# Shifts of attention maxima moved from VectorE to GpSimd under a new hand-written order, and the feature rows of the prologue turned earlier

## The chip, the cores and the metric

The kernel runs on one core of a Trainium2 chip. The metric is the time of one launch on the device in microseconds (us), the median over several runs. A profile of one execution gives every instruction on the engines: TensorE (PE, with its weight loads shown apart as PEld), VectorE (DVE), ScalarE (ACT), GpSimd (POOL), and the queue of the SyncE (SP), which issues nearly all DMAs.

## The reference: what is computed

One trunk layer runs on a group of 128 context tokens and a group of 512 latent tokens with shared weights, all in float32:

```python
def trunk_layer(h, ada, p, rope_tabs, ctx_k, ctx_v):
    sh1, sc1, g1, sh2, sc2, g2 = jnp.split(ada, N_ADA, axis=-1)
    u = rms_norm(h, p["g_pre1"]) * (1 + sc1) + sh1
    mo, k, v = mixer(u, p, rope_tabs, ctx_k, ctx_v)
    h = h + g1 * rms_norm(mo, p["g_post1"])
    u = rms_norm(h, p["g_pre2"]) * (1 + sc2) + sh2
    h = h + g2 * rms_norm(conv_ffn(u, p), p["g_post2"])
    return h, k, v
...
    def one_block(qblk):
        s = jnp.einsum('bqkgd,btkd->bkgqt', qblk, k).astype(jnp.float32) * scale
        p = jax.nn.softmax(s, axis=-1).astype(v.dtype)
        return jnp.einsum('bkgqt,btkd->bqkgd', p, v)
```

`ada` is `silu(c) @ w_ada + b_ada`, six vectors of 1024 for each group. The mixer projects `u` with `w_in`, normalises q and k per head, turns the latent ones by a two-axis rotary, attends (16 query heads, 4 key heads of 64; latent tokens read 512 latent and 128 cached keys, context tokens only the 128 context keys), adds a gated short convolution, and multiplies by `w_o`. A gated feed-forward part of width 2816 follows.

## The kernel before

**Arithmetic.** A matrix product in float32 is made of three products of parts: each operand is cut into an upper part `hi` in a shorter format and a rest `lo`, and `hi*hi + hi*lo + lo*hi` is summed in PSUM. The upper part of a weight is copied by ScalarE (`hi`, L826), the rest subtracted in two halves by VectorE or GpSimd (`lo`, L831).

**Prologue** (L374 to L687, up to about 57 us of the trace). SP loads five tiles of 128 token rows (`XT`), then the first columns of `w_ada` and of `w_in`. ScalarE's own queue loads `rows1`: c, the context vector, the bias `b_ada` and `g_pre1` as 72 rows of 128. TensorE begins with `WARM` = 32 turns of the unit matrix (L379), whose output nobody reads. For each tile t, `square(t)` sums squares on ScalarE (L435) and takes the root on GpSimd (L282, L283), `normal(t)` scales the tile on VectorE (L440), `x_turn(t)` turns its eight blocks on TensorE (L447), and `x_copy` takes the two halves out of PSUM on ScalarE or VectorE (L453, L455). `features()` (L416) turns `rows1` on TensorE (L418) and makes silu of c and of the context vector on ScalarE (L419, L420); `feature_columns()` (L423) copies the turned rows into `feat` on VectorE and adds 1 to two of its groups (L424, L426). `ada1_mm` (L478) multiplies silu(c) with the columns of `w_ada`; its results set `scsh`, with which `modulate` makes `u`. PE, ACT, DVE and SP run here in the order in which the code is written.

**Attention** (L747 to L1233, about 57 to 228 us). Every piece of work has a number in order of its making, a name, an engine (`ways`), the works that it follows and the buffers that it takes. `PLAN` is a text of 944 items, number, letter and digits: the letter picks the way (`a` the first engine, `b` the second, `c` the third), the digits the buffers. `follow` (L722) issues the works in that order, and each engine's own order follows from it; nothing is rearranged later.

- Query tile `qgt` (key head g, tile t): four quarters of six matmuls (`qgt.0` to `.3`, L709), rotary products on VectorE (L849, L850) and a sum of the two (`add`, L870, either engine), squares on ScalarE (L872), sums on VectorE (L874), a factor on GpSimd (L877), the norm (L892, either engine), two turns on TensorE (`qgt turn`, L1034), upper part on ScalarE (L1036) and rest on VectorE (L1038). Key tiles go the same way (norm L882).
- The values are scaled (`v scale`, L975) and cut into halves (L981, L984).
- 36 steps: one for each key head's context tile (n = 0, 9, 18, 27) and two for each of its four latent tiles, with two heads in each. In a step with latent tokens: scores of both heads (`s n`, twelve matmuls, L1073), the negated maximum of each head (L1120, VectorE), for the second head the maximum shifted by 15 ln 2 (L1123), the exponential on ScalarE with that bias and its sum (L1128), the first float16 half of the weights on ScalarE (L1134), the second half (L1139 for the second head, L1141 for the first), a transposing DMA of both halves by SP (L1145), and the value product (`pv n`, L1162 and L1170). Then come the output's scaling and cut (L1182 to L1192).
- `POOL_WAY` has a digit for each of the 32 latent steps: with 1, the second head's exponential goes to a buffer in SBUF and its second half is made by GpSimd; with 0, both stay in PSUM and on VectorE.
- TensorE fills the time between scores and value products with quarters of later query tiles and with two columns of gates.

**Behind it** come the product with `w_att_out`, the other columns of `w_in` and the later products (L1274), in a fixed order, up to the end.

Of the kernel before, what the change touches and what calls it, by code (L numbers as in the profile page):

```python
# [18 lines left out]
ALU = mybir.AluOpType  # L19
# [26 lines left out]
WARM = 32  # L46
# [5 lines left out]
71a0 15a 21a 80a 36a 5b0 31a 72a2 81a 45a 52a3 7a 16a 37b1 82a 22a12 92a2 46a 85a1 73a 8a0 23b 83a10 17a2 54a3 9a 86a 132a 38a1  # L52
10a 27a3 42a01 18a0 39a 93a 55a 19a 43a 40a 28a4 74a 60b2 94a 29a 59b3 95a 87a 75b 20a 105a3 98a0 84a 30a 76a1 106a 88a 77a0 99a
78a 107a 100a 58b4 56a0 47b4 65a 347a2 57a 134b 61a 96a22 48a1 63a 348a 108a 97a 49a 118a0 349a 101a 109a01 119a 133b 50a 89a2
102a1 120a 62a 90a1 209a 111a2 351a1 91a 110a 121a 112a 138a 66a 113a 359a10 352a 124a1 103a2 114a 122a10 204a 353a5 365a 140b
115a4 135a0 116a3 366a 104a 367a0 139b 136a 117a 350a 360a 368a0 373a20 123a 275a 125a 361a 64a 126a 141a 362a4 379a 205b 142a
380a 371a 363a 381a1 354a1 369a 143a2 364a0 382a2 374a 391a10 355a2 144a0 356a 383a 375a 151a0 370a1 145a 397a 357a 152a 376a1
146a 398a 385a 384a2 392a 399a0 153a 377a 147a 393a 154a 358a 206b 405a02 394a3 378a3 155a01 400a4 395a 127a 148a1 157a2 411a
401a 149a0 128a3 372a0 396a4 129a1 412a 158a 413a1 130a 159a 406a 414a0 423a12 403a 402a5 150a 407a 415a 164a1 429a 408a2 165a
156a 430a 281a 409a 431a0 166a 416a0 160a 424a 432a1 167a 417a 425a 433a 437a02 168a20 426a3 435a 386a 170a1 443a 169a 410a1  # L60
444a 427a 177a1 387a2 445a1 388a 178a 438a 389a 428a2 446a4 455a12 390a 171a 439a 447a 404a0 456a 440a0 434a3 449a 457a 441a
172a 418a 461a 458a2 173a 161a2 442a4 419a1 179a 459a 162a2 180a 163a 462a 420a 463a0 469a10 448a5 181a10 464a3 467a 182a 487a2
470a 183a0 421a 465a 190a1 460a0 488a 471a 191a 475a 472a1 192a 422a 210a 184a 466a1 174a0 473a 193a 185a 175a3 489a 176a 476a
186a 194a02 450a0 211a 436a 212a 477a1 474a4 490a 195a 478a0 481a 499a10 196a2 907a 479a 451a1 197a 207a1 491a4 505a 276a 208a
198a 506a 480a5 452a 507a0 492a 213a 199a 500a 453a 513a20 508a2 493a2 454a 278b 501a 468a0 514a 509a 502a3 519a 515a 214a 503a
277b 510a3 516a1 482a 520a 215a2 521a1 517a 187a3 504a0 483a0 511a 525a 531a02 188a1 484a 522a0 189a 518a1 200a3 216a1 523a 537a
485a 494a1 201a0 486a 538a 217a 223a0 495a2 202a 524a4 218a 539a0 496a 224a 532a 497a 219a 540a4 545a12 498a 533a 911a 541a
220a1 551a 534a2 225a 221a2 552a 226a 535a 542a5 553a1 546a 554a3 563a02 227a11 547a 555a 536a2 222a 548a1 557a 512a1 569a 229a0
228a 570a 549a 571a0 526a 556a0 564a 572a0 577a12 543a 230a 527a0 573a 565a 528a 550a3 236a0 583a 529a 566a4 231a 237a 575a 584a
578a 585a1 238a 574a1 567a 232a 586a2 239a 530a 579a 587a 595a20 240a02 568a4 580a3 589a 544a1 242a2 601a 241a 602a 596a 558a  # L70
603a0 588a2 581a 597a 233a0 243a 609a01 234a3 607a 244a 559a1 582a5 235a 604a1 560a 249a0 610a 245a 561a 598a0 250a 562a 605a
611a 599a 246a1 251a 247a1 615a 600a0 612a4 627a2 616a 248a 617a1 252a 628a 606a3 618a2 590a1 621a 613a 255a1 619a 629a 256a
576a 253a20 614a2 257a 254b 639a10 591a2 620a5 630a 631a3 592a 258a 262a0 640a 593a 263a 594a 641a 645a 264a 282a 646a 632a 265a
647a0 633a1 283a 279a1 266a11 284b 642a0 280a 648a1 643a 653a20 267a 915a 268a0 651a 908a 644a4 269a 649a 608a0 654a 659a 655a
622a 270a 909a 650a0 656a4 259a3 660a 271a 661a1 285a 657a 910b 260a0 286a 665a 623a0 658a3 261a 662a2 272a2 624a 671a21 287a0
625a 663a 288a2 626a 273a2 289a 634a1 919a 677a 290a 664a2 295a0 678a 635a2 672a 679a0 291a 296a 274a 673a 636a 685a10 637a 683a
674a3 638a 297a 691a 680a0 298a 681a 692a 675a 693a1 292a1 299a21 676a5 694a1 703a20 686a 300a 301a1 293a3 302a 666a0 695a 687a
682a1 709a 688a4 697a 294a 652a 710a 303a 704a 696a2 711a0 689a 308a1 667a0 304a 705a 668a 717a01 690a3 669a 715a 712a2 670a
309a 706a3 723a 713a 310a 724a 707a 725a1 311a 718a 714a0 726a0 305a0 735a21 312a12 306a1 727a 719a 307a 708a4 684a0 314a0 741a
720a1 313a 742a 721a 698a 743a0 728a1 736a 744a4 749a01 729a 699a1 315a 745a 722a5 737a 700a 321a1 750a 738a2 322a 755a 316a  # L80
751a 746a2 323a 739a 752a3 317a 324a 756a 747a 701a 753a 757a1 767a2 740a3 702a 327a2 716a0 758a0 768a 759a 328a 769a 325a00
779a01 754a0 761a 329a 326b 318a1 780a 730a 319a0 760a4 771a1 330a 320a 781a 772a 334a1 785a 782a4 331a4 335a 773a1 332a2 786a
770a 783a 787a 336a 333a 912a 337a 791a 784a5 793a02 340a1 914a 788a2 338a22 913b 916a 799a 762a1 339a 731a1 800a 732a 801a0
917b 748a 789a 733a 341a 802a3 790a0 918b 811a21 734a 794a 763a0 342a 920a0 764a 795a 817a 921a 803a 765a 796a0 818a 812a 922a
819a1 797a 923a 343a 804a4 813a 766a 825a10 805a 924a 823a 814a1 798a2 774a1 820a4 831a 821a 344a0 832a 815a 833a0 826a 816a3
345a3 843a20 834a2 346a 827a 835a 792a0 822a1 849a 775a2 828a3 850a 776a 806a 851a1 836a0 829a 777a 844a 857a01 807a1 852a0 778a
808a 830a5 845a 925a1 853a 863a 809a 926a 846a1 864a 810a 858a 865a0 927a 854a2 837a 855a 928a 859a 847a 930a0 860a4 869a 848a4
875a12 929a 861a 866a2 824a1 867a 881a 882a 876a 838a 883a 862a1 877a 931a 868a3 878a3 887a 932a 839a0 879a 884a0 933a 889a01
880a0 885a 934a 840a 856a0 841a 895a 886a5 896a 842a 935a2 897a 890a 898a1 936a 891a 899a 937a 892a4 901a 900a2 938a 943a 893a
# [23 lines left out]
def trunk_layer(ctx, tc, x_prompt, x_sample, cache_k, cache_v, c, c_ctx, w_ada, b_ada, g_pre1, g_post1, g_pre2,  # L113
# [260 lines left out]
    with tc.tile_pool(name="pro", bufs=2) as pro, tc.manual_schedule(engines={mybir.EngineType.SP}):  # L374
        warm = pro.tile([128, 1], F32, name="warm", bufs=1)
        S.activation(warm, mhalf[:, 0:1], AF.Silu)
        wps = ps1()
        for _ in range(WARM):
            PE.transpose(wps[:, 0:128], ident, ident)  # L379

        def load_rows(srcs, eng):
# [34 lines left out]
        def features():  # L416
            ptr = ps1()
            PE.transpose(ptr[:, 0:72], rows1, ident[0:72, 0:72])  # L418
            S.activation(svec[:, :, 30], ptr[:, 0:8], AF.Silu)  # L419
            S.activation(svec[:, :, 31], ptr[:, 8:16], AF.Silu)  # L420
            return ptr

        def feature_columns():  # L423
            V.tensor_copy(feat[:, 0:72], ptr1[:, 0:72])  # L424
# [293 lines left out]
    def also(w, eng, do):  # L718
        w.ways.append((eng, do))
        return w  # L720
# [26 lines left out]
    with tc.tile_pool(name="att", bufs=1) as at:  # L747
# [305 lines left out]
        for n, (g, t, pi) in enumerate(steps):  # L1053
# [52 lines left out]
            else:  # L1106
                pts[n], exs = [], []
                for h in hs:
# [10 lines left out]
                    def most(s_of=s_of, mk=mk, h=h):  # L1119
                        V.tensor_reduce(out=mk[:, h:h + 1], in_=s_of(), axis=AX.X, op=ALU.max, negate=True)  # L1120

                    def shifted(mk=mk):
                        V.tensor_scalar(out=mk[:, 1:2], in0=mk[:, 1:2], scalar1=SHIFT * math.log(2), scalar2=None, op0=ALU.add)  # L1123
# [3 lines left out]
                    ex = work(f"exp{n}.{h}", "ACT",  # L1127
                              lambda s_of=s_of, e_of=e_of, mk=mk, h=h: S.activation(e_of(), s_of(), AF.Exp, bias=mk[:, h:h + 1],  # L1128
                                                                                   accum_out=mk[:, 4 + h:5 + h]), [mx], [ar[h]] + [er] * way)
# [1395 lines left out]
```

## Time and profile before

| | |
|---|---|
| median of 3 runs | 1075.21 us (1074.77 to 1075.44) |
| profiled execution, own time | 1074.79 us |
| its span in the trace | 1073.0 us |
| PE busy | 1056.8 us (98%) |
| DVE busy | 899.9 us (84%) |
| ACT busy | 598.4 us (56%) |
| POOL busy | 133.1 us (12%) |
| granted TensorE clock over the span | 0.999 |

The span is the trace's first to last instruction; what lies around it is 1.79 us. An engine's busy time counts its computing instructions; matmuls overlap each other, so a busy TensorE can still hold short waits. "Busy" rows by stretch have for each engine the busy time and the number of instructions, then the granted clock, the DMA engines' busy share and GB/s. Wait rows have the waiting engine and line, what released it, the sum in us, how often, and the longest. Rows of one line have the shortest, median and longest time in ns.

### The profile page before, as it was taken

To read this page: it belongs to the slowest core of one execution; us is meant where nothing else is said; L and a number is where in the kernel's file an instruction comes from. 1 tells how busy PE (TensorE), PEld (TensorE's weight loads), DVE (VectorE), ACT (ScalarE), POOL (GpSimd) and SP (SyncE) were. 2 spreads that over 40 slices of the span, in tenths; PEclk is the share of its full clock that TensorE was granted. 3 is DMA by queue.
4 is the path that set the end of the run, shared out by engine and by line. 5 is a ranking of instruction groups with operands and counts; after the bars stand their busy time and mean duration, and the time that the engine had idled before them with its cause. 6 is when DMAs were issued, how large, how long until landed. Compare 5 with 4: busy or idle time off the path is not lost.

```text
span 1073.0 us, 20652 instructions
## 1 busy us (share of the span) xinstructions
PE 1056.8 (98%) x8216; PEld 995.4 (93%) x8216; DVE 899.9 (84%) x1379; ACT 598.4 (56%) x1057; POOL 133.1 (12%) x162
## 2 busy tenths in 40 slices
PE   8999999999999999999999999999999999999997
PEld 6788898899999999999998789999999999999996
DVE  5699999865498999896599678889999988989897
ACT  5478999942344544445322366645555555546673
POOL 1087676500000000000000020000000000000001
PEclk9999999999999999999999999999999999999999
DMA  9829999962244333223668634434544534436873
GB/s 320 256 82 175 190 168 187 191 147 60 75 123 124 93 103 94 79 79 99 189 188 253 198 131 129 121 116 136 166 131 152 150 122 131 152 116 219 277 275 115
DMA packets 243197, 164.02 MB, mean 153 GB/s; under 512 B 94874, under 2 KB 216214, under 8 KB 243102
## 3 DMA queue, kind: packets, MB, share of 16 engines
q1 hardware_dynamic: 242990, 162.68, 55.5%
q8 instruction: 64, 1.05, 0.4%
q14 instruction: 31, 0.25, 0.1%
q10 hardware_dynamic: 112, 0.04, 0.0%
HBM read 123.31 MB, written 17.36 MB: 131 GB/s over the span
## 4 chain that ended last, share of the span: by engine, by line
PE 90%; DVE 3%; ACT 2%; DMA 1%; POOL 1%; issue 1%; SPq 1%; DVEq 0%; ACTq 0%; POOLq 0%
PE b L1274 47%; PE b L235 10%; PE b L237 10%; PE b L236 9%; PE s L709 4%; PE s L1073 2%; PE s L1170 2%; PE s L235 1%; PE s L237 1%; PE s L1162 1%; PE s L478 1%; DVE marks L1120 1%; PE s L236 1%; PE b L1900 1%; ACT P L1134 1%
## 5 line engine op out<-in xcount | busy, mean ns | idle before, releaser
L1274 PE MATMUL b<-ZBr,whi 128*128 128x320 f32 x688 | 152.1, 309 | 0.0
L1274 PE MATMUL b<-MT,whi 128*128 128x320 f32 x608 | 134.4, 309 | 0.0
L1274 PEld LDWEIGHTS b<-ZBr,whi 128*128 128x128 f32 x688 | 114.9, 188 | 0.1
L1274 PE MATMUL b<-ZBr,wlo 128*128 128x320 f32 x344 | 106.1, 308 | 0.0
L1274 PEld LDWEIGHTS b<-MT,whi 128*128 128x128 f32 x608 | 101.7, 188 | 0.0
L1274 PE MATMUL b<-MT,wlo 128*128 128x320 f32 x304 | 94.0, 309 | 0.0
L1261 ACT ACTIVATE whi<-SUM 128x1024 fp32r<-128x1024 f32 x40 | 42.2, 1055 | 78.3 <-DVE SUM L1813 75.7
L1843 DVE SCALAR_TENSOR_TENSOR Y<-C,cffn,Y 128x642 f32<-128x642 f32 x88 | 77.9, 886 | 0.9
L1261 ACT ACTIVATE whi<-WB 128x1024 fp32r<-128x1024 f32 x38 | 40.2, 1058 | 55.5 <-DVE WB L1368 55.5
L1274 PE MATMUL b<-ZBT,whi 128*128 128x320 f32 x320 | 71.0, 308 | 0.0
L1274 PE MATMUL b<-UL,whi 128*128 128x320 f32 x228 | 70.8, 311 | 0.0
L1274 PE MATMUL b<-UH,wlo 128*128 128x320 f32 x228 | 70.1, 307 | 0.0
L1274 PE MATMUL b<-UH,whi 128*128 128x320 f32 x228 | 69.7, 306 | 0.0
L1282 ACT ACTIVATE p<-b 128x320 f32<-128x320 f32 x78 | 34.1, 437 | 55.3 <-PE b L1274 53.5
L1274 PEld LDWEIGHTS b<-ZBr,wlo 128*128 128x128 f32 x344 | 64.6, 188 | 0.0
L1265 DVE TENSOR_TENSOR wlo<-raw,whi 128x1024 fp32r<-128x1024 f32 (+1 forms) x51 | 50.4, 1020 | 13.4 <-ACT whi L1261 13.4
L1274 PEld LDWEIGHTS b<-MT,wlo 128*128 128x128 f32 x304 | 57.1, 188 | 0.0
L1274 PEld LDWEIGHTS b<-ZBT,whi 128*128 128x128 f32 x320 | 54.2, 188 | 1.6
L1120 DVE TENSOR_REDUCE marks<-s 128x1 f32<-128x640 f32 x64 | 52.1, 817 | 4.0 <-PE s L1073 3.8
L1265 DVE TENSOR_TENSOR wlo<-WB,whi 128x1024 fp32r<-128x1024 f32 x38 | 46.5, 1224 | 8.8 <-ACT whi L1261 8.7
L2355 POOL TENSOR_TENSOR ssqs<-ssqs 128x1 f32<-128x1 f32 x4 | 1.4, 356 | 412.9 <-ACT GJ L2349 412.9
L1261 ACT ACTIVATE whi<-raw 128x1024 fp32r<-128x1024 f32 (+1 forms) x51 | 43.5, 892 | 15.4 <-DMA raw<-in_w_o_dram 12.5
(477 smaller groups left out, 3348.1 us busy)
## 6 DMA issues: line engine op xcount, KB each, us to landing
raw<-in_w_in_dram SPq DMA_DIRECT2D x48, 512.0 KB
RAW<-in_w_up_dram SPq DMA_DIRECT2D x40, 512.0 KB
raw<-in_w_down_dram SPq DMA_DIRECT2D x22, 512.0 KB
GA<-in_w_ada_dram SPq DMA_DIRECT2D x16, 512.0 KB
actd<-Y SPq DMA_DIRECT2D x18, 321.0 KB
actl<-ACTb SPq DMA_DIRECT2D x18, 321.0 KB
A<-actl SPq DMA_DIRECT2D x9, 642.0 KB
A<-actd SPq DMA_DIRECT2D x9, 642.0 KB
```

Source lines behind the costliest of these rows:

```text
L235: PE.matmul(out, ah, bh, start=start, stop=False)
L236: PE.matmul(out, ah, bl, start=False, stop=False)
L237: PE.matmul(out, al, bh, start=False, stop=stop)
L709: PE.matmul(out, a, b, start=start and n == 0, stop=stop and n == 2, skip_group_check=True)
L1073: PE.matmul(o[h], q_of(hl, i, rows), kk[kx][rows, g, ks], start=m == 0, stop=m == 2, tile_position=(64 * h, 0), skip_group_check=True)
L1120: V.tensor_reduce(out=mk[:, h:h + 1], in_=s_of(), axis=AX.X, op=ALU.max, negate=True)
L1170: PE.matmul(p[64 * h:64 * h + 64, i * 128:i * 128 + 128], VH[:, w, s, vc_], src, start=k == 0 and m == 0, stop=k == ks[-1][0] and m == 2, ...
L1261: S.activation(to[0], raw, AF.Copy)
L1265: V.tensor_tensor(out=lo, in0=raw, in1=hi.bitcast(F32), op=ALU.subtract)
L1274: PE.matmul(out, p[:, ws], q[:, k, :], start=start and k == 0 and n == 0, stop=stop and k == 3 and n == 2, skip_group_check=True)
L1282: S.activation(t, pair[j][b], AF.Copy)
L1843: V.scalar_tensor_tensor(out=y, in0=crows(j)[i][:, d:d + NACT], scalar=cffn[:, 44 * d + o:44 * d + o + 1], in1=y, op0=ALU.mult, op1=ALU.add)
```

## The change

The order `PLAN` is another one throughout (944 items again); in it, 20 of the 32 shifts carry the letter `b`. `shifted` takes the engine as an argument and has GpSimd as its second way. In `POOL_WAY`, two digits become 1. In the prologue, `features()` stands ahead of the last eight warming turns and of the first tile's norm, and `feature_columns()` right behind the first tile's norm; the number of warming turns is 32 as before.

```diff
 PLAN = """
-67a0 44a0 12a00 203a 24a1 137a 34a2 68a 25a 13a 0a 32a11 131a 2a1 69a 11a 26a 6a 3a 41a 33b 70a 14a1 35a 51a2 4a 1a3 79a1 53a4
...
-939a 894a4 940a 870a 888a1 871a2 872a 902a 873a 874a 941a 903a1 904a 942a 905a 906a
+67a0 11a 32a00 137a 44a0 203a 2a1 22a11 68a 33a 14a2 131a 51a2 12a32 69a 41a 21a 3a 13a 70a 31a 15a 24a1 1a4 34a2 4a 79a1 25a 0a
...
+871a1 872a 900a4 938a 873a 874a 939a 940a 888a0 902a 941a 903a2 904a 942a 905a 906a
 """
-POOL_WAY = "11111111111111111111111101111100"
+POOL_WAY = "11111111111111111111111111111110"
...
-        for _ in range(WARM):
+        for _ in range(WARM - 8):
             PE.transpose(wps[:, 0:128], ident, ident)
...
         for t in range(2):
             square(t)
+        ptr1 = features()
+        for _ in range(8):
+            PE.transpose(wps[:, 0:128], ident, ident)
         normal(0)
+        feature_columns()
         square(2)
         x_turn(0)
         normal(1)
         square(3)
-        ptr1 = features()
         x_turn(1)
...
         x_copy(2, 0)
-        feature_columns()
         x_copy(1, 1)
...
-                    def shifted(mk=mk):
-                        V.tensor_scalar(out=mk[:, 1:2], in0=mk[:, 1:2], scalar1=SHIFT * math.log(2), scalar2=None, op0=ALU.add)
+                    def shifted(eng, mk=mk):
+                        eng.tensor_scalar(out=mk[:, 1:2], in0=mk[:, 1:2], scalar1=SHIFT * math.log(2), scalar2=None, op0=ALU.add)
                     mx = work(f"max{n}.{h}", "DVE", most, [sc], [ar[h]])
                     if h:
-                        mx = work(f"shift{n}", "DVE", shifted, [mx])
+                        mx = also(work(f"shift{n}", "DVE", lambda f=shifted: f(V), [mx]), "POOL", lambda f=shifted: f(G))
```

The two plans read by the works' names, TensorE's order in the opening and at the end, first before, then after (`s` scores, `pv` value products, `g` quarters of the gates):

```
before  q03.3 q04.0 q04.1 q01t q02t q04.2 q04.3 s1 q03t q10.0 q10.1 s2 q10.2 q10.3 pv0 s3 q11.0-3 s4 q10t q04t pv1 s5
after   q03.3 k4t q04.0 s0 vb q04.1 q01t q04.2 q04.3 s1 q10.0 q10.1 q02t s2 q10.2 q03t q10.3 s3 pv0 q11.0 q11.1 s4 q11.2 q11.3 q12.0-2 s5 q04t q10t
...
before  s34 pv30 pv31 g0 2.1-3 s35 pv32 g1 0.0-3 g1 1.0 g1 1.1 pv33 pv34 pv35 g1 1.2 g1 1.3
after   s34 pv31 pv30 s35 g0 2.1-3 g1 0.0 g1 0.1 pv32 pv33 g1 0.2 g1 0.3 g1 1.0 g1 1.1 pv34 pv35 g1 1.2 g1 1.3
```

GpSimd's order up to q03's norm (f = factor):

```
before  k1 add, k2 f, k0 f, k3 f, k1 f, k4 f, k1 norm, k2 norm, k4 add, q00 f, q01 f, q01 add, q01 norm, q02 f, lo 10, q02 add, q02 norm, lo 10, q03 add, q03 f, q03 norm
after   k3 add, k1 add, k0 f, k2 f, k3 f, k3 norm, k4 add, k1 f, k1 norm, q00 f, q01 f, k4 f, q02 f, v scale 1, v scale 2, q01 norm, q03 f, v lo 2, lo 10, q04 add, shift1, q02 norm, q04 f, lo 11, q03 norm
```

More of the change, by code (lines that the diff above doesn't have):

```diff
@@ L55 @@
[L55 to L70, printed above, removed]
@@ new lines @@
+35a 72a1 6a 80a 23b 26a 45a 81a 71a0 5b0 36a 82a 27b1 53a4 7a 8a3 85a2 42a10 37a2 28a2 9a 92a0 83a12 29a 43a 10a 38a4 52a0 93a
+16a 84b 39a 30a 94a 132a 40a 17a3 95a 73a 86a 54a1 74a 98a0 134a 96a21 105a3 87a 55a 106a 58b3 46a 99a 107a 75b 97b 18a2 100a
+47b4 76a4 19a 108a 59a0 77a0 20a 48a0 111a1 118a1 78a 49a 60a2 109a00 347a0 50a 56a4 88a 61a 112a 119a 65a 110b 113a 57a 62a 63a
+89a3 120a 90a1 66b 348a 138a 121a 91a 349a 359a21 64a 122a12 133b 365a 123a 135a0 209a 124a2 360a 351a4 366b 101a 136a 367a0
@@ new lines @@
+130a 430b 401a 431a1 150a 386a1 168a12 432a0 424a 437a10 159a 170a2 402a0 425a 171a 372a 172a 169b 443a 426a4 416a3 427a 177a0
+444b 433a 445a0 438a 178a 428a1 446a3 435a 455a20 173a 387a1 439a 388a 447a 179a 389a 434a2 456a 440a2 180a 457a 390a 449a 160a
+461a 404a1 458a1 462a 441a 463a1 418a 448a0 459a 464a4 469a10 181a20 419a2 465a 442a4 420a 183a0 161a4 470a 421a 190a0 162a2
+182a 475a 466a3 471a 191a 422a 192a 472a0 163a 476b 184a 477a0 487a2 473a 185a 460a5 436a1 478a3 488a 186a 210a 467a 481a 174a2
@@ new lines @@
+479a 474a1 193a 175a3 489a 176a 450a 194a01 212b 499a10 480a2 211a 196a1 451a2 207a0 490a 491a2 505a 276a 907a 208a 492a 506b
+507a1 452a 213a 277b 493a0 197a 500a 453a 513a20 508a4 198a 454a 501a 195b 482a1 514a 199a 502a1 511a 509a 519a 468a 515a 503a
+516a0 214a 520b 510a4 278b 521a0 517a 187a3 215a1 188a0 531a20 518a1 216a2 189a 483a0 217a 522a3 484a 494a0 218a 537a 485a 504a2
+200a3 495a2 486a 525a 523a 201a1 538a 223a1 496a 539a1 202a 224a 532a 911a 497a 540a2 524a3 545a10 498a 219b 533a 541a 220a0
@@ new lines @@
+245a 612a4 599a 252a 606a2 616b 613a 617a0 246a1 627a2 253a10 618a0 639a10 628a 255a2 614a4 619a 247a0 576a0 645a 629a 248a 646b
+590a 640a 254a 620a1 256a 262a1 641a 630a 621a 257a 607a 631a2 263a 600a3 642a1 258a 632a 264a 647a1 643a 265a 282a 651a 644a0
+259a4 266a22 653a01 591a1 283b 268a0 592a 260a1 622a1 654a 593a 633a5 648a4 284b 269a 908a 608a 261a 594a 270a 267b 655a 279a0
+909a 915a 659a 271a 623a0 280a 656a0 624a 660b 285a 649a 657a 625a 661a0 286a 658a1 272a4 662a3 626a 671a01 287a0 910b 273a2
@@ new lines @@
+665a 288a1 650a4 274a 634a1 677a 663a 295a0 678a 635a1 289a 919a 679a1 636a 290a 296a 664a2 672a 637a 680a1 685a21 638a 291b
+673a 681a 292a1 691a 674a2 297a 293a3 692a 298a 675a 693a0 682a3 294a 301a2 686a 703a01 694a0 299a12 687a 695a 676a5 652a1 709a
+688a4 666a 710a 300a 711a1 689a 696a0 704a 717a21 667a0 712a3 668a 683a 697a 669a 308a0 302a 713a 705a 723a 690a4 309a 706a1
+715a 718a 724b 310a 303a 725a0 707a 714a1 311a 719a 670a 735a10 304a 312a21 720a2 729a 313a 314a0 708a2 305a1 726a0 741a 684a0
@@ new lines @@
+306a0 721a 742b 727a 743a1 698a 736a 722a3 744a4 307a 749a20 315a 699a2 745a 737a 700a 321a1 728a5 750a 738a3 316a 322a 751a
+739a 323a 755a 317a 752a1 740a0 324a 701a 753a 756b 757a0 767a1 325a00 318a4 746a4 758a2 702a 768a 319a1 730a0 759a 327a1 320a
+769a 761a 747a 779a02 328a 754a3 326b 329a 334a1 780a 771a0 760a5 335a 785a 781a 336a 772a 786b 782a3 330b 337a 787a1 783a 331a3
+716a 912a 338a11 770a 791a 339b 340a2 793a20 913a 788a4 784a1 341a 731a2 789a 748a1 332a2 799a 916a 773a2 800a 762a 333a 801a0
@@ new lines @@
+917b 732a 794a 790a0 733a 811a10 802a1 342a 734a 918a 763a0 795a 920a0 817a 803a 796a2 921a 764a 805a 765a 797a 922a 818b 804a4
+914b 819a1 812a 923a 820a3 825a20 766a 798a3 343b 924a 821a 813a 344a1 831a 774a0 345a3 814a0 346a 832b 822a5 823a 833a0 792a1
+815a 834a4 826a 816a2 843a01 775a1 835a 827a 776a 806a 849a 777a 828a1 778a 836a0 850a 844a 925a0 851a1 837a 829a 926a 852a2
+807a2 830a1 857a12 853a 845a 808a 809a 927a 846a3 863a 854a3 928a 864a 810a 865a0 847a 930a1 929a 858a 875a20 848a4 866a0 855a
```

32 lines of the change are left out of this document (10 added, 22 removed).

## Prediction

> **What bounds the kernel now.** I read first the busy time of each engine in stretches, then who waited for whom on TensorE and on ScalarE in the attention, then the chain of waits, and last the single operations that the change moves. The stretches (TensorE, weight loads, VectorE, ScalarE, GpSimd):
>
> ```profile
> 0.00:17.00 17.00, 12.96 (x111) 11.18 (x113) 8.14 (x18) 9.98 (x20) 5.36 (x19) 1.00 0.96 302
> ...
> 57.00:77.00 20.00, 19.64 (x182) 18.70 (x182) 19.38 (x46) 15.01 (x38) 18.84 (x20) 1.00 0.19 54
> 77.00:92.00 15.00, 13.18 (x145) 11.45 (x147) 14.12 (x33) 13.18 (x30) 14.84 (x14) 1.00 0.84 167
> 92.00:130.00 38.00, 37.36 (x526) 33.50 (x521) 34.19 (x76) 35.11 (x82) 25.05 (x26) 1.00 1.08 185
> 130.00:180.00 50.00, 49.51 (x744) 44.79 (x742) 46.65 (x105) 45.76 (x107) 33.50 (x32) 1.00 1.11 181
> 180.00:228.00 48.00, 46.51 (x700) 42.69 (x699) 36.30 (x79) 38.99 (x91) 17.82 (x16) 1.00 1.05 175
> ```
>
> From 57 to 228 us, the attention, TensorE is busy 166.20 of 171 us, so 4.8 us is the most that an order without waits can win, unless records hide more; 1.82 us of it lies in the 15 us from 77 on. VectorE and GpSimd are near full up to 92 us, and later VectorE and ScalarE stay around nine tenths. Everything behind 228 us follows in a fixed order, so a time won here moves the end by as much. Which waits these are:
>
> ```profile
> PE s L1034 <- POOL QF L892: 1.8, 2, 1.1
> PE s L1073 <- DVE P L1141: 0.8, 2, 0.6
> PE s L1162 <- DVE QT L1038: 0.5, 1, 0.5
> PE s L1170 <- DMA PT<-P: 0.4, 1, 0.4
> ...
> PEld s L1034 <- POOL QF L892: 2.3, 2, 1.3
> ...
> PEld s L1073 <- DVE P L1141: 1.5, 3, 0.8
> PEld s L1162 <- DVE QT L1038: 1.0, 2, 0.7
> ...
> ACT E L1128 <- DVE marks L1123: 3.4, 8, 0.8
> ...
> ACT s L1128 <- DVE marks L1123: 1.7, 2, 1.0
> ```
>
> The two waits of the turn of a query tile (L1034) for GpSimd's norm (L892) are the largest; behind them come single waits for VectorE. ScalarE waits ten times, 5.1 us in all, for the shift of a maximum (L1123), which the change moves. The chain through the opening and at the end:
>
> ```profile
> 78.07 0.44 POOL QF L892
> 78.64 2.53 POOL wlo L831 x2
> ...
> 84.61 2.74 POOL P L1139 x2
> ...
> 90.23 0.58 POOL QF L892
> ...
> 221.97 3.35 DMA PT<-P
> 225.36 1.03 PE s L1170 x30
> ```
>
> In the opening GpSimd's queue sets the end; at the end the transposing DMA of the last step's weights does, with TensorE out of filler work.
>
> **The prologue: nothing, between -0.2 and +0.5 us.** Its rows:
>
> ```profile
> 1.69 5.84 PE L379 MATMUL s<-ident 128*128 128x128 f32 x32 [1.69 <-POOL ident masks.py:199]
> 7.57 1.09 PE L447 MATMUL s<-ident,xn 128*128 128x128 f32 x8
> L418 PEldq EVENT_SEMAPHORE x2: 51/51/51, 7.6 to 7.8; - x2
> 12.29 0.23 DVE L424 COPY feat<-s 128x72 f32<-128x72 f32 x1
> 12.77 0.82 PE L447 MATMUL s<-ident,xn 128*128 128x128 f32 x6
> ...
> 14.45 1.07 PE L478 MATMUL s<-araw,s 128*32 128x128 f32 x28 [0.52 <-DMA araw<-in_w_ada_dram]
> ```
>
> TensorE's sequencer stood at its last semaphore for the feature rows at 7.8 us (the third row), though the turn of these rows came only after the first tile; I read it as their landing. In the new order eight of the 32 warming turns stand behind that turn, so TensorE runs 24 of them until some 6.1 (24/32 of the 5.84) to 6.6 us (all but eight at the warm pace), waits to 7.85 and does the turn; the last eight, at the warm pace of a tile's turn (eight in some 0.9 us of loads, 1.09 with the drain), end near 8.8. The first tile's turn then starts 1.2 to 1.3 us later than 7.57. Queued behind the waiting turn are all tile turns; VectorE's copies of the tiles wait for them, and ScalarE's two short activations of the features now wait ahead of the third square. What covers it is the first product with the modulation weights, which waits for their DMA until 14.45 whatever stands before it. The fourth tile's turn ended by 13.6 (12.77 + 0.82); delays shrink along the way, because the later tiles wait for their own rows and norms, and I get about 14.0 for the end of the fourth. VectorE wins back 0.4 us at 12.29, where the feature copy and its two additions go, and the new place for them lies in its wait for the second norm. If the cover were gone the 1.25 us would show; I take +0.0.
>
> **The operations of the attention.** Rows that price what is moved:
>
> ```profile
> L1123 DVE TENSOR_SCALAR marks<-marks x32: 144/154/155, 79.2 to 216.7; 128x1 f32<-128x1 f32 x32
> L282 POOL TENSOR_SCALAR var<-ssq x5: 190/362/402, 5.9 to 12.0; 128x1 f32<-128x1 f32 x5
> L1139 POOL TENSOR_TENSOR P<-E,P x29: 1397/1408/1418, 84.6 to 210.5; 128x640 f16<-128x640 f32 x29
> L1139 DVE TENSOR_TENSOR P<-s,P x3: 816/825/825, 192.5 to 218.6; 128x640 f16<-128x640 f32 x3
> L870 POOL TENSOR_TENSOR QF<-QF,X x14: 718/730/1250, 68.8 to 191.6; 128x256 f32<-128x256 f32 x14
> L870 DVE TENSOR_TENSOR QF<-QF,X x2: 426/528/630, 148.2 to 184.5; 128x256 f32<-128x256 f32 x2
> L892 POOL TENSOR_TENSOR QF<-QF,rq x19: 609/613/616, 69.6 to 197.2; 128x256 f32<-128x256 f32 x19
> L892 DVE TENSOR_TENSOR QF<-QF,rq x1: 421/421/421, 67.9 to 67.9; 128x256 f32<-128x256 f32 x1
> L877 POOL TENSOR_TENSOR rq<-ssqs,mhalf 128x4 f32<-128x4 f32 x20 | 21.3, 1067 | 3.9 <-DVE ssqs L874 3.8
> L831 POOL TENSOR_TENSOR wlo<-raw,whi x13: 1271/1289/1805, 71.2 to 193.6; 128x512 fp32r<-128x512 f32 x13
> L831 DVE TENSOR_TENSOR wlo<-raw,whi x5: 681/693/1221, 112.0 to 189.8; 128x512 fp32r<-128x512 f32 x5
> ```
>
> Counted in the two plans: to GpSimd go 20 of the 32 shifts, the second half (L1139) of two more steps, two of the three value scalings, one lower half of the values and one sum of a key tile; to VectorE go six rotary sums, six norms of query tiles and one half of a weight's lower part. VectorE loses 20 x 0.154 + 2 x 0.825 + 3 x 0.69 + 0.42 = 7.2 us and gets 6 x 0.43 + 6 x 0.42 + 0.69 = 5.8: 1.4 us less on 151 busy. GpSimd gets 20 x 0.36 + 2 x 1.41 + 3 x 1.29 + 0.73 = 14.6 and loses 6 x 0.73 + 6 x 0.61 + 1.29 = 9.3. A shift on GpSimd is not in the trace; the nearest row is the one-column operation of L282, 0.19 to 0.40 us. GpSimd's own queue has room behind 92 us (76 of 136 busy) and none before. TensorE's instructions are the same, and the scores stand at almost the same places of its queue, so its 166 us stay.
>
> **The opening.** The turns of q03 and q04 are the two that wait. q03's stands three quarters of a tile's product, a score step and a tile's turn later, counted from step 1's scores; q04's three quarters and a score step later, and its norm runs on VectorE. Prices from the chain:
>
> ```profile
> 65.95 0.71 PE s L709 x6
> ...
> 96.71 1.08 PE s L1073 x12
> ```
>
> That is 3 x 0.71 + 1.08 = 3.2 us more cover for each (and q03's 0.2 more). But GpSimd has more ahead of q03's norm: two value scalings and a lower half (3 x 1.29), two sums (2 x 0.73), a factor (1.07, L877) and a shift (0.36), less three sums (2.2): 4.6 us, or 1.2 beyond the cover, less what it idles now. So q04's wait (the longer, 1.1 us of 1.8) goes, and q03's stays or grows by at most 1.2. I take -1.0, between 0 and -1.8.
>
> **The middle and the end.** The other waits in the windows are 4.8 - 1.8 = 3.0 us by busy time; the weight loads, which see a wait earlier than the pipelined matmuls do, have 2.5 us for the two VectorE causes shown against 1.3 on TensorE. VectorE has 1.4 us less to do, and the maxima of a pair no longer have the shift between them, so the next score area comes free 0.15 us sooner, twenty times. I take -1.8, between 0 and -3.0. At the end the order puts step 35's scores some three quarters (2.1 us) earlier before the last value product, so the DMA that lands at 225.3 is covered: -0.4, the wait on TensorE, between 0 and -0.6.
>
> **The shift's price.** On GpSimd the exponential of the second head gets its bias later: 0.36 instead of 0.154, and a hand-over between engines twice instead of once. No row shows such a pair, so I bound it: 0 where ScalarE has other work (22 of 32 steps now), and 20 x 0.4 = 8 us if each were on the path. Ten of 32 wait now; 20 x 10/32 x 0.3 = 1.9 us on ScalarE, which idles 16 us in the 136 behind 92 us; a quarter of it, 0.5, reaches TensorE.
>
> **Sum.** 0 - 1.0 - 1.8 - 0.4 + 0.5 = -2.7 us. The profiled execution took 1074.79 us, its span being 1073.0, and gives 1072.1; the median of the runs is 0.42 above that execution, so **1072.5 us**. The forecast's own range is 1071.2 to 1073.9.
>
> **Rivals.**
> *All waits go* (0.12): all 4.8 us, 1070.4. For it speaks that the waits are few and single; against it that GpSimd's opening queue is longer.
> *The maxima keep the pace* (0.16): up to 92 us VectorE is busy 33.50 of 35 us, and its work ahead of step 5's maxima is unchanged by my count, so TensorE's won time is waited off at the scores; only the end and some half a microsecond remain: 1074.3.
> *The shift behind a long GpSimd operation* (0.16, the slower side): a shift that finds a second half (1.41) or a weight's lower part (1.29) running waits for it; then the exponential, the half, the DMA and the value product are late in turn. GpSimd is busy 76 of 136 us, so a shift met at random waits 0.56 x 0.7 = 0.4 us, and with the 0.3 above each costs 0.7, 14 us for 20; it decides from the point where more than 3.2 us of that reaches TensorE (the 2.7 won, and the 0.5 that the sum has already). If half of it does, 7 - 3.2 = 3.8 and the time is 1079.0; if 5 us do, 1077.0, which I take. For it: ScalarE has waited for this value ten times already. Against: the order can place a shift ahead of the long operation.
> *Two engines on one port* (0.06): the twelve sums and norms that come to VectorE read two tiles in SBUF. The rows of L831 and L870 show such operations at 1.22 instead of 0.69 and at 0.63 instead of 0.43, and on GpSimd 1.25 instead of 0.73. With 0.3 us each, 12 x 0.3 = 3.6 us more on VectorE, 2.2 net of its 1.4; half of that on the path is 1.1, and the middle's 1.8 is lost: -2.7 + 1.8 + 1.1 = +0.2, or 1075.4. The Trainium skill, "SBUF — State Buffer", section "SBUF: two separate sides", says that the two engines take a shared port pair exclusively, and the loser blocks for the whole instruction, if VectorE's has two SBUF inputs. The largest values of these rows agree with it; by it an operation met at random behind a second half would lose up to 1.41 us. The medians do not show it, so by the trace its chance is small.
> That the change doesn't do what it says is excluded by the count; it can only do it at no effect, which is the second rival.
>
> **How the numbers follow.** The forecast has 0.50. What this measurement can tell from no change is about 0.2%, or 2.15 us: below 1073.06 is faster. Of the forecast 0.44 lies below that, with the first rival 0.56 faster. Same: 0.06 of the forecast, 0.16, and 0.04 of the port's: 0.26. Slower: 0.16 and 0.02: 0.18. The range goes from 1070.5, the bound by TensorE's idle time, to 1075.8, leaving out the slower rival's far side and the part of the first rival below it.
>
> **What would show it.** Right: TensorE's wait for L892 below 1 us, its busy time from 57 on unchanged in less time, no wait for the last DMA, the first modulation product at 14.4 to 14.6. Wrong: ScalarE's waits for L1123, now on GpSimd, over 10 us; VectorE's sums (L870) above 0.6 us on the mean; q03's turn waiting over 2 us; scores waiting for L1141 more than now. A time above 1075.8, or a first modulation product that waits for something else than its DMA beyond 14.9, would make the prediction wrong.

## The result and the profile after

| | before | after |
|---|---|---|
| median of 6 runs | 1074.99 us | 1079.29 us (1078.33 to 1082.81) |
| ratio, 95% interval | | 1.0042 (1.0032 to 1.0053) |
| profiled execution, own time and span | 1074.79, 1073.0 us | 1079.82, 1078.0 us |

The changed kernel is slower by 4.3 us; 1072.5 was predicted. Its lines from the attention on are numbered 2 higher. The stretches after (TensorE, weight loads, VectorE, ScalarE, GpSimd; then the granted clock):

```profile
57.00:77.00 20.00, 19.59 (x180) 18.58 (x180) 19.31 (x47) 13.04 (x30) 19.02 (x18) 1.00 0.16 47
77.00:92.00 15.00, 13.32 (x124) 11.18 (x123) 13.86 (x27) 13.79 (x34) 14.29 (x17) 1.00 0.82 154
92.00:130.00 38.00, 37.57 (x533) 33.29 (x531) 34.04 (x75) 35.71 (x83) 26.69 (x30) 1.00 1.04 189
130.00:180.00 50.00, 49.67 (x746) 44.97 (x746) 45.97 (x98) 46.72 (x108) 34.48 (x37) 1.00 1.06 183
180.00:228.00 48.00, 44.48 (x621) 40.19 (x620) 36.70 (x76) 39.17 (x89) 18.22 (x18) 0.96 1.05 169
```

Up to 180 us TensorE is as busy as before. In the last stretch it idles 3.5 us (before 1.5), and the clock falls to 0.96. The starts of the scores, read from the two traces, place the loss (us against before; "end" is the attention's last weight load, 228.09 before; the other columns are experiments below):

```
            after  loads behind  key norm on ScalarE  norms first
step 1      -0.13     +0.23            -0.03             +0.55
step 8      +0.79     +1.00            +1.23             +2.09
step 17     +0.43     +0.62            +0.85             +1.78
step 27     +0.65     +0.85            +1.15             +2.05
step 31     +1.04     +1.27            +1.57             +2.45
step 34     +1.84     +0.91            +1.20             +2.10
end         +4.91     +0.56            +0.92             +1.82
```

Step 1 moves from execution to execution, mostly by some tenths, so differences down a column count: 0.9 us are lost up to step 8, nothing from there to step 27, 0.4 up to step 31, and 3.9 from there to the end. Each column is one execution. The waits of TensorE and ScalarE in the attention:

```profile
PE s L1172 <- DMA PT<-P: 1.8, 1, 1.8
PE s L1075 <- ACT E L1130: 1.3, 2, 1.1
PE s L711 <- POOL wlo L833: 1.0, 1, 1.0
...
PE s L1036 <- POOL QF L894: 0.4, 1, 0.4
```

```profile
...
ACT E L1130 <- POOL marks L1125: 2.0, 6, 0.5
ACT P L1136 <- DMA PT<-P: 1.6, 1, 1.6
...
ACT s L1130 <- DVE marks L1125: 0.9, 1, 0.9
```

The turns' waits for GpSimd's norm went from 1.8 to 0.4, and ScalarE waits 2.0 us for shifts on GpSimd. New are ScalarE's wait for a transposing DMA (1.6) and the size of TensorE's (1.8, before 0.4); both stand in the chain at the end:

```profile
202.20 7.11 DMA PT<-P
...
209.39 0.37 ACT P L1136
209.77 4.57 DMA PT<-P
214.33 0.04 issue
214.38 1.05 PE s L1172 x30
```

Call T30.1 the transposing DMA of step 30's second head. It is issued at 202.20 and takes 7.11 us; until it lands, its weight buffer (the tile `P`) is not free, ScalarE cannot write the weights of step 32's first head (209.39), and behind this the scores of step 34 come 1.1 us late. Step 31's own transposes stand behind it in SP's queue; the last of them is issued at 209.77, and the value product of step 31 waits 1.8 us for it. What stands ahead of T30.1 in SP's queue, after and then before:

```profile
195.86 1.32 SPq L217 DMA_DIRECT2D raw<-in_w_att_out_dram  x1
197.29 4.15 SPq L1147 DMA_TRANSPOSE PT<-P  x2
201.49 0.61 SPq L217 DMA_DIRECT2D raw<-in_w_att_out_dram  x1
202.20 3.09 SPq L1147 DMA_TRANSPOSE PT<-P  x1
```

```profile
191.70 0.37 SPq L217 DMA_DIRECT2D raw<-in_w_att_out_dram  x1
193.42 2.13 SPq L1145 DMA_TRANSPOSE PT<-P  x1
195.65 1.22 SPq L217 DMA_DIRECT2D raw<-in_w_att_out_dram  x1
```

Two loads of 512 KB, the third and fourth column block of `w_att_out`. They go into raw buffers (the landing places of weights as loaded) that come free with the lower parts of units 17 and 18; a unit is one block of weights, numbered in the order of loading. Before, these lower parts were done by 194.85, and both loads were issued ahead of step 29's transposes. In the new order the last half of unit 17's stands behind step 30's shift on GpSimd, and the second load goes out between the transposes of steps 29 and 30:

```profile
197.34 0.22 POOL L1125 TENSOR_SCALAR marks<-marks 128x1 f32<-128x1 f32 x1
197.64 1.28 POOL L833 TENSOR_TENSOR wlo<-raw,whi 128x512 fp32r<-128x512 f32 x1
```

### The profile page after: what moved, and what is told of

Read it like the earlier page. It is cut to its first block, busy times and chain, and to the rows that moved or that the text cites. A ratio compares the mean times of both kernels' runs of the same rounds, so it can differ in the third digit from the quotient of the medians.

```text
span 1078.0 us, 20634 instructions
## 1 busy us (share of the span) xinstructions
PE 1060.6 (98%) x8216; PEld 997.6 (93%) x8216; DVE 900.2 (84%) x1366; ACT 600.4 (56%) x1057; POOL 136.1 (13%) x175
## 4 chain that ended last, share of the span: by engine, by line
PE 86%; DVE 4%; ACT 3%; DMA 2%; issue 2%; POOL 2%; SPq 0%; DVEq 0%; ACTq 0%; POOLq 0%
PE b L1276 47%; PE b L235 10%; PE b L237 9%; PE b L236 9%; PE s L711 3%; PE s L1075 2%; PE s L1172 1%; DMA PT<-P 1%; ACT P L1136 1%; PE b L1902 1%; PE s L478 1%; PE s L1164 1%; DMA araw<-in_w_ada_dram 1%; DVE P L1143 1%; DVE marks L1122 1%
```

## Experiments

"Before" beside a result is the kernel before in the same set of runs.

**The prologue alone.** The new prologue with the old order.

> The kernel before with the changed prologue alone; order, shifts and everything else as before. Theory (the loss is at the end of the attention, where two 512 KB loads fall between the last transposing DMAs): the prologue does nothing, 1075.0 us within 0.4, and step 1's scores start at 76.7 to 76.9 us. Rival (the prologue makes the stages behind it late): 1076 us or more.

1074.96 us (before 1074.96; ratio 1.0002, 0.9993 to 1.0011), step 1 at 0.11 behind. The prologue does nothing that can be measured, as predicted.

**The shifts alone, in both orders.** In the new order all back on VectorE; in the old order the same 20 on GpSimd:

```diff
 changed kernel, in PLAN
-366b 380b 398b 412b ...
+366a 380a 398a 412a ...
 kernel before, in PLAN
-366a 380a 398a 412a ...
+366b 380b 398b 412b ...
```

> The changed kernel with all 32 shifts on VectorE, each at its place in the order. Theory (late loads): still 1078.3 to 1079.8 us, with ScalarE's wait for the 1.6 us DMA at about 209 us and TensorE's wait for the last transposes still there. Rival (GpSimd makes the biases late or its queue too long by the shifts): 1075 to 1076.5 us.

> The kernel before, its own order and prologue, with the same 20 shifts on GpSimd. Theory (late loads): 1075 to 1076.5 us, since a shift costs 0.22 us on GpSimd and its order behind is unchanged. Rival (shifts on GpSimd are what costs): 1078 us or more, ScalarE waiting over 5 us for the shifted maxima.

1083.01 us (ratio 1.0069, 1.0054 to 1.0085), and 1084.44 (1.0091, 1.0076 to 1.0106). Both expectations of the theory fall: in the order of before the move costs 9.5 us, in the new order taking it back costs 3.7. So a shift's price is its place in an engine's queue, which the order sets. In the new order with the shifts on VectorE, ScalarE waits for them 7.1 us (3.1 for all shifts in the changed kernel):

```profile
ACT E L1129 <- DVE marks L1124: 7.1, 11, 1.8
```

That execution was the fastest of its four (1080.41); in it the scores of step 31 start 1.9 us later than in the changed kernel. How the rest of the 3.7 comes about was not followed. Waits of ScalarE, GpSimd's timeline and one exponential in the old order with shifts on GpSimd:

```profile
ACT E L1127 <- POOL marks L1122: 12.1, 13, 1.9
```

```profile
82.82 1.04 POOL L876 TENSOR_TENSOR rq<-ssqs,mhalf 128x4 f32<-128x4 f32 x1
83.84 1.27 POOL L830 TENSOR_TENSOR wlo<-raw,whi 128x512 fp32r<-128x512 f32 x1
85.19 0.22 POOL L1122 TENSOR_SCALAR marks<-marks 128x1 f32<-128x1 f32 x1
```

```profile
85.45 0.79 ACT L1127 ACTIVATE E<-s,marks 128x640 f32<-128x640 f32 x1 [1.87 <-POOL marks L1122]
```

The maximum was there at 83.43 (82.61, 0.82 long); the shift stood behind a factor and a weight's lower part, and ScalarE waited 1.87 us. This is the mechanism of my slower rival, at full size (it had 14 us of waits on ScalarE, of which half reach TensorE); the new order avoids most of it.

**The loads behind the transposes.** Three works more; the last two issue the loads by the order (the first finds its load already issued):

```diff
+        for u in (19, 20, 21):
+            def late(u=u):
+                state["limit"] = u + 1
+                fetch(u + 1)
+            work(f"load {u}", "SP", late)
 in PLAN
-296a 664a2
+296a 944a 664a2
-900a4 938a
+900a4 945a 946a 938a
```

> The changed kernel, the loads of the third and fourth column block of w_att_out (read only at 284 us) issued by SP behind the last transposing DMA of the attention instead of among those of steps 28 to 30; nothing else moves. Theory (late loads): the second half of step 30's transposes lands 5 us after its issue or less instead of 7.1, ScalarE does not wait 1.6 us for a weight buffer, the waits of step 34's scores and of step 31's value product (1.2 and 2.0 us) shrink below 0.5 each, the clock stays whole: 1075.0 to 1076.5 us. Rivals (shifts on GpSimd; the order of TensorE at the end, without filler): 1078.3 to 1079.8 us.

1075.58 us (before 1074.96; ratio 1.0001, 0.9989 to 1.0013): 3.7 of the 4.3 us are gone. The ratio does not tell the rest from nothing; by the medians 0.6 us stay, as in the profiled execution, whose attention ends 0.56 late. Its last stretch, and SP's issue of T30.1 with T30.0, then of T31.1:

```profile
180.00:228.00 48.00, 47.29 (x703) 42.88 (x702) 37.24 (x77) 39.71 (x91) 18.46 (x19) 1.00 1.04 169
```

```profile
200.98 2.97 SPq L1147 DMA_TRANSPOSE PT<-P  x2
...
204.84 1.95 SPq L1147 DMA_TRANSPOSE PT<-P  x1
```

T30.1 is issued 1.2 us earlier, the first two need 2.97 us of SP instead of 6.06 (202.20 to 208.26), and T31.1 goes out 3.5 us earlier than in the changed kernel (208.39). Step 31's value product starts at 211.34 with no wait, and the clock is 1.00. One thing in the expectation is wrong: the trace has ScalarE cut these blocks from 233.9 us on, not from 284; that is still more than 30 us behind their issue. Then the second load alone (945 ahead of step 29's transposes, 946 where it is above):

> The changed kernel with the second of the two loads alone behind the last transposes, the first where it stands (ahead of step 29's). Theory (the second load, between step 29's and step 30's transposes, is the one that costs): 1075.2 to 1076.2 us, no half clock. Rival (both are needed to move): 1077 us or more.

1076.15 us (1075.01 to 1079.27; before 1074.93), the profiled one 1075.73 with no half clock: by the median the load between the transposes is the one that costs. Four of the twelve executions still took 1077.6 to 1079.3; what happens in them no trace shows.

**The loads put among the transposes of the old order.** Works 944 to 946 as above, at the places that the changed kernel gives the loads.

> The kernel before, with the two 512 KB loads put where they stand in the changed kernel: one ahead of step 29's transposing DMAs, one between step 29's and step 30's (two and one places later than before; the order of all else is that of before). If the place of the loads is enough by itself: step 30's and 31's transposes issue 2 to 3 us later, ScalarE waits for a weight buffer, 1077 to 1079 us. If it takes the new order too (the last value products come without filler work ahead of them): 1075.0 to 1076.0 us. Rival (the loads have nothing to do with it): 1074.7 to 1075.3 us, with transposes no later than before.

1076.14 us (before 1074.60; ratio 1.0012, 1.0002 to 1.0021), between two expectations: ScalarE waits 1.7 us for a weight buffer, as in the changed kernel, but from 180 us on no wait of TensorE is above 0.6 us, and the clock is whole. The profiled execution is the slowest of the ten (1078.03); 1.3 us of its loss lie ahead of step 1, and 1.65 between step 31 and the end. The place costs about 1.5 us by itself (0.2 to 2.3 by the interval); in the new order the loads cost 3.7.

**Filling the wait.** Three quarters of the gates ahead of step 31's value product (931, 932 and 933 ahead of 838); and, by itself, twelve turns there whose output the product overwrites:

```diff
                 p = at_bank(pvr)
+                if n == 31:
+                    for _ in range(12):
+                        PE.transpose(p[:, 128 * pi:128 * pi + 128], ident, ident)
```

> The changed kernel, with three quarters of the gates (2.1 to 2.3 of the first gate column) moved ahead of step 31's value product on TensorE, where the order before had them ahead of step 35's scores; the loads stay where they are. Theory (the late transpose makes TensorE idle twice within 5 us, and half the clock for 3.4 us follows): the 1.96 us wait is covered, the clock is whole, the wait of step 34's scores (1.2) stays: 1076.0 to 1077.5 us. Rival (the late transposes hold ScalarE and the later steps anyway, so the wait only moves behind step 35): 1078.0 to 1079.5 us.

> The changed kernel, with twelve turns of the unit matrix (whose output the product overwrites) ahead of step 31's value product on TensorE: they take some 1.3 to 1.5 us of the 1.96 us in which it waits for the last late transpose, and move no other work. Theory (TensorE's share of work in a stretch of 3.4 us decides on the clock of the next): the value product starts no earlier, the clock stays whole, and 1.5 us of the loss goes: 1077.2 to 1078.2 us. Rival (the lower clock has nothing to do with the wait, or costs nothing): 1078.8 to 1079.8 us, a stretch of half clock still in the trace.

The gates did not help, against both expectations: 1080.13 us (before 1074.60). The twelve turns may have: 1078.06 (1077.29 to 1078.62; before 1074.75), 1.2 less than the changed kernel, though the intervals of the two ratios overlap (1.0018 to 1.0041, and 1.0032 to 1.0053). In the profiled execution the product also starts 0.9 us sooner (213.48 instead of 214.38), because its transpose landed sooner, so what the clock alone is worth this run does not show. TensorE by stretches of 3.41 us, in the changed kernel, with the gates, and with the turns:

```profile
208.43:211.84 3.41, 2.31 (x23) 2.13 (x22) 2.08 (x5) 2.44 (x6) 0.00 (x0) 1.00 1.17 245
211.84:215.26 3.42, 1.63 (x41) 1.26 (x39) 2.60 (x5) 3.13 (x6) 1.43 (x2) 1.00 1.11 179
215.26:218.67 3.41, 3.41 (x50) 3.24 (x46) 0.49 (x1) 1.16 (x3) 1.37 (x1) 0.50 1.14 140
```

```profile
207.92:211.34 3.42, 2.01 (x17) 1.83 (x17) 1.77 (x5) 1.77 (x5) 0.00 (x0) 1.00 1.24 232
211.34:221.58 10.24, 10.24 (x100) 9.56 (x101) 3.25 (x7) 3.91 (x8) 2.80 (x2) 0.50 0.63 116
```

```profile
211.25:214.66 3.41, 3.41 (x62) 3.00 (x60) 2.71 (x7) 3.27 (x7) 1.40 (x1) 1.00 1.11 181
214.66:218.08 3.42, 3.42 (x57) 3.14 (x53) 1.83 (x5) 2.14 (x5) 1.41 (x1) 1.00 1.12 158
```

Where TensorE worked 1.63 of 3.42 us, the next stretch ran at half the clock; 3.41 us at half the clock are 1.7 us lost, by estimate. With the gates moved the stretch with the wait of step 34's scores, which lies ahead of them, was followed by it too (2.01 of 3.42), and half the clock lasted 10.24 us; why so long is open. That profiled execution (1084.87) is 4.7 us above its median and the slowest of its five. With the turns the stretch is full and the clock stays.

**The lower part earlier.** The last half of unit 17's lower part ahead of unit 18's on GpSimd (914 ahead of 917); both loads then stand ahead of step 29's transposes.

> The changed kernel, with the last half of the lower part of the seventeenth unit's weights moved on GpSimd's queue from behind the shift of step 30 to ahead of the first half of the eighteenth's, so that both raw buffers come free by about 196.5 us and both loads stand ahead of step 29's transposes. Theory (the second load, released late, is what lands among the transposes): step 30's transposes are issued 2 us earlier than in the changed kernel, 1075.5 to 1077.0 us. Rival (GpSimd's queue at this place is what counts; a later factor of q34 and a later second half of step 29 cost as much): 1078.5 us or more.

1078.91 us (1076.86 to 1081.04; before 1074.60). In the profiled execution (1076.86) both late waits are gone, but on GpSimd the last query tile's factor starts 1.2 us and step 30's shift 1.6 us later (196.00 and 198.96); step 31's scores wait 1.0 us for the exponential behind that shift, and the turn of the last query tile comes 1.5 us later: the place moves the loss as the rival said. It settles little.

**The opening.** With the loads behind, the norm of key tile k1 on ScalarE; then two norms of query tiles earlier in GpSimd's queue as well:

```diff
-17a3
+17c3
 second kernel, in PLAN, two norms moved
-133b 365a 123a ... 366b 101a
+133b 365a 101a 123a ... 366b
-140b 350a 361a 104a 379a 362a3 114a
+114a 140b 350a 361a 104a 379a 362a3
```

> The changed kernel with the two loads behind the last transposes, and the norm of one key tile (k1) made by ScalarE in four activations, at its place in the order, instead of by GpSimd (1.04 us there). Theory (GpSimd's queue sets the changed opening): the wait of q10's second quarter for the lower part of its weights, 1.2 us, falls below 0.4, step 8's scores come 0.6 to 1.0 us earlier than with the loads moved alone, and the time is 1074.6 to 1075.0 us. Rival (VectorE's maxima keep the pace of the opening): the wait goes but step 8 starts no earlier, 1075.4 to 1075.8 us.

> The changed kernel with both loads behind the last transposes, the key norm on ScalarE, and two norms of query tiles earlier in GpSimd's queue: q02's ahead of q04's sum and of step 1's shift, q03's ahead of the second half of the lower part of the eleventh unit. Theory (a shift in GpSimd's queue makes the norms behind it wait for VectorE's maximum): the waits of q02's and q03's turns (1.5 and 0.55 us in the kernel with the key norm on ScalarE) fall below 0.5 together, step 8's scores come 0.7 to 1.2 us earlier, 1074.4 to 1075.2 us. Rival (VectorE's maxima keep the pace of the opening): the waits go over into waits of scores, step 8 as late as now, 1075.5 to 1076.0 us.

1075.85 us (before 1074.75), and 1076.46 (before 1074.93). Neither is faster than with the loads moved alone (1075.58). The wait is handed on each time; TensorE's, in the one and in the other:

```profile
PE s L1036 <- POOL QF L894: 1.5, 2, 1.2
```

```profile
PE s L1075 <- ACT E L1130: 1.1, 1, 1.1
```

From the lower part of a weight it goes to the turn of q02, whose norm stands behind a shift, and from there to step 2's scores, which wait for the area that step 1's exponential reads, which waits for VectorE's maximum. GpSimd's queue alone was not the bound. VectorE's first maxima of steps 1 and 2 are 3.41 us apart before (78.38, 81.79) and 3.89 after (78.55, 82.44); what the new order puts between them:

```profile
80.35 0.67 DVE L1103 TENSOR_TENSOR P<-s,P 128x512 f16<-128x512 f32 x1
80.94 0.67 DVE L833 TENSOR_TENSOR wlo<-raw,whi 128x512 fp32r<-128x512 f32 x1
...
82.09 0.42 DVE L1040 TENSOR_TENSOR QT<-s,QT 128x256 fp32r<-128x256 f32 x1 [0.39 <-ACT QT L1038]
```

Other work has left this place (a shift, the rest of q03 and a half of the values' rest), and VectorE waits 0.39 us for ScalarE at 82.09. With the norms first that wait is gone and the distance is still 3.71 (79.78 to 83.49). So VectorE's new order may explain some 0.3 us of the opening's 0.9; no run has put it back, and the rest is open.

The opening of norms first, with the second load alone behind, was tried for a faster version:

> The two together: the opening with the norms first and the second load alone behind. If the opening's theory holds and two loads right behind the attention delay what follows: 1074.0 to 1074.9 us. If the opening is VectorE's: 1075.3 to 1076.0 us.

1077.68 us (before 1074.93): none.

**Joined orders.** The old order up to step 8 and the new one behind; the old one up to step 28 and the new one behind; the same with the second load behind.

> The order of before up to step 8's scores, the changed order behind it, with the changed prologue (the shifts of steps 1 to 8 are then on VectorE). Theory (the changed opening costs 0.8 to 1.0 us at step 8, by GpSimd's longer queue; the end costs the rest): 1078.0 to 1078.8 us, step 9 on 0.2 to 0.4 us behind before's places instead of 0.7. Rival (the loss is in the opening): 1075 to 1076 us.

> The order, shifts and prologue of before up to step 28's scores, the changed order behind them (with three of the twenty shifts on GpSimd); the two loads fall where they fall in the changed kernel. Theory (the end's order with its late loads is the loss, the opening adds 0.8): 1077.5 to 1079.0 us, with the waits before step 34's scores and step 31's value product. Rival (the loss needs the late opening or the shifts of the middle): 1074.5 to 1076.0 us.

> The same, with the second load behind the last transposing DMA. Theory (without the late load the changed end is 0.4 to 0.7 us better than the end before, and the opening's loss is left out): 1074.2 to 1075.0 us, the attention's end at or before 228.1 us. Rival (the changed end needs what stands ahead of it): 1075.5 us or more.

1083.68, 1079.64 and 1079.59 us (before 1074.60, 1075.06, 1075.06). These three do not decide what they were made for: each seam brings waits of its own. In the first, ScalarE waits 2.75 us for a weight buffer at 109.7 and TensorE 3.4 for ScalarE; in the others the turn of q33 waits 1.4 to 1.5 us at 188 and step 31's scores 1.3 to 1.9. In these moving the second load behind won nothing (1079.64 and 1079.59), so what a late load costs differs with the order around it. That the opening costs 0.9 rests on the starts of the scores; the first of these runs has step 8 within 0.1 of its own step 1.

**The kernel before, mended.** The loads behind; and with them the key norm on ScalarE.

> The kernel before, with the same two loads behind its last transposing DMA. If the loads among the transposes cost nothing in the order of before, as its trace has it (no wait over 0.7 us there): 1074.6 to 1075.2 us. Rival (they cost there too): 1073.5 to 1074.5 us.

> The kernel before, with the loads behind and the norm of the key tile k1 on ScalarE, ahead of the first key tile's copies. If GpSimd's queue sets the opening of before as well: the waits of q03's and q04's turns (0.8 and 1.4 us) shrink, 1073.8 to 1074.6 us. If VectorE keeps its pace: 1074.8 to 1075.2 us.

1075.37 and 1076.10 us (before 1074.75). In the profiled execution of the first the attention ends 0.47 us earlier, the wait for the last transpose being gone, but the time is no better (ratio 1.0007, 0.9998 to 1.0017), above both expectations; where that goes was not followed. No kernel of the study is faster than the one before.

## Why the prediction was wrong

- **The prologue (0): right.** Rows after:

```profile
7.79 0.26 PE L418 MATMUL s<-ident,rows 72*128 72x72 f32 x1 [0.72 <-DMA rows<-in_g_pre_dram]
7.89 1.04 PE L561 MATMUL s<-ident 128*128 128x128 f32 x8
8.76 1.99 PE L447 MATMUL s<-ident,xn 128*128 128x128 f32 x16
```

The first tile's turn starts 1.2 us later, and the fourth tile's ended at 13.86, where I had 14.0; the cover held.
- **The opening (-1.0): wrong, +0.9.** The two waits that I named did shrink, from 1.8 to 0.4 us. The step failed that took nothing else as waiting: the longer queue of GpSimd, which I had set against these turns alone, makes a quarter of q10 wait 1.0 us for a weight's lower part, and where a run took that wait away, the next one appeared, for a norm and then for VectorE's maxima. My second rival (the maxima keep the pace) comes near this; VectorE's work between the maxima, which I took as unchanged, may account for some 0.3 us; that the rest is handed from wait to wait is read from the traces, and no run has removed it.
- **The middle (-1.8): wrong, about -0.1** (step 8 to step 27). I turned VectorE's 1.4 us less work and TensorE's short waits into time won; from 92 to 180 us TensorE is busy 87.24 us and was busy 86.87 before, so at most 0.4 us of its waits went there. The 0.4 us from step 27 to step 31 were not followed.
- **The end (-0.4): the step that failed.** It followed TensorE's order and took the DMA's landing from before. Its own mechanism holds once the loads are away: step 31 to the end is then 0.7 us shorter. But I had counted the lower parts of weights for GpSimd's and VectorE's load only, not for what they release: two loads on SP, which the plan does not list. They cost 3.7 us, the half clock that follows the waits included (1.7 by estimate); at the same places in the old order they cost 1.5. Which part of the new order makes the difference no run has shown: moving the gates' quarters back did not help.
- **The shift's price (+0.5): no cost in this order.** Rows of the moved operations after:

```profile
L1125 POOL TENSOR_SCALAR marks<-marks x20: 207/221/237, 79.9 to 200.8; 128x1 f32<-128x1 f32 x20
...
L872 DVE TENSOR_TENSOR QF<-QF,X x8: 404/418/580, 64.2 to 191.0; 128x256 f32<-128x256 f32 x8
L894 DVE TENSOR_TENSOR QF<-QF,rq x7: 405/415/417, 69.9 to 198.9; 128x256 f32<-128x256 f32 x7
```

0.22 us each, not 0.36; ScalarE's waits for shifts fell from 5.1 to 3.1 us, and the shifts taken back to VectorE made the kernel slower. The third rival's time (1077.0) lay nearest, and its half case (1079.0) comes close to the result, but by luck: its mechanism hardly shows in this kernel (2.0 us of waits for shifts on GpSimd) and is at work in the old order.
- **The shared port: not seen** in what was moved; sums and norms on VectorE have medians of 0.42.

## What to carry to other kernels

Who moves a piece of work must follow what it releases, not only who waits for its result: here a buffer came free 7 us later (198.92 against 191.67), and a transfer that nobody needed for 30 us went out among those that everything waited for. The price of a small operation on another engine's queue is what stands ahead of it there: the same 20 shifts cost 9.5 us in one order and saved 3.7 in another. And a wait of under 2 us can cost nearly twice, when half the clock follows it (here 1.8, and 1.7 by estimate).

## What the hardware showed

- The granted clock changes in stretches of 3.41 us. Half the clock followed stretches in which TensorE worked 1.63 of 3.42 us (longest gap 1.8) and 2.01 of 3.42, and in the joined orders 0.43, 1.50 and 2.02 of 3.41; stretches of 1.80, 1.88 and 2.03 in other executions or places were not followed by it. What decides is open; the grid stands elsewhere in each execution, and a wait can fall across two stretches:

```profile
206.63:210.04 3.41, 1.80 (x37) 1.71 (x37) 2.35 (x7) 2.86 (x6) 1.07 (x2) 1.00 1.21 177
210.04:213.46 3.42, 3.42 (x33) 3.06 (x31) 1.60 (x5) 1.61 (x5) 0.47 (x1) 1.00 1.04 198
```

These are the shifts on VectorE in the new order. The Trainium skill, "TensorE: Matmul & The Clock Gate", section "Part 1: The HAM clock gate (the "warmup" mystery)", has the clock fall to half after an idle window of about 3.4 us, free-running. The stretch's length agrees; here none of these stretches was idle throughout, and 1.4 to 1.9 us without work in a stretch were enough in four cases, and 1.4 to 1.6 us were not in three others.
- A transposing DMA right behind a 512 KB load took 3.09 us of SP's queue and 7.11 to land (in the old order with the loads put there, the one behind the load 2.75 and 6.88); with both loads behind T30.1 took 1.35 and 5.1, with the second load behind 1.60 of the queue. What slows it is not shown.
